# Constant fills on VectorE, and the input's buffers on the right-hand side of SBUF, in a hybrid decoder layer

## The chip, the cores and the metric

The kernel runs on one core of one Trainium2 chip. The metric is the device time of one execution in microseconds (us); lower is better. The engines are TensorE (PE in the profile, its weight loads PEld), VectorE (DVE), ScalarE (ACT), GpSimd (POOL) and SyncE (SP), which here issues nearly all DMAs.

## What is computed

One decoder layer over 512 tokens of width 1024, in float32. RMSNorm of the input x, one combined input projection `h @ w_in`, then three token mixers side by side (sparse attention over compressed, selected and window keys; a chunked spatial-gating MLP; RWKV-7 time mixing), each with a SiLU gate and its own output projection, merged by sigmoid gates, one output projection, a gated per-layer embedding, and a final RMSNorm. The part that the change touches is the beginning:

```
h = _rmsnorm(x, norm_g[i])
proj = h @ w_in[i]
nkc, nvc = ...                       # keys and values for compression, columns of proj
def _compress(kv, w1, w2, pe):
    blk = kv[:, idx] + pe            # blocks of 32 tokens, stride 16
    hid = silu(einsum('bnlgd,ldh->bngh', blk, w1))
    return einsum('bngh,hd->bngd', hid, w2)
```

## The kernel before

The kernel splits every float32 operand of the large projections into a high and a low half, so that each block takes three products: weights' high half by the activations' high half, the same weights by the activations' low half, and the weights' low half by the activations' high half. `wload` (L67 to L80) brings 256 KB of weights into a raw tile `wr` (4 buffers), ScalarE casts it to `wh` (L78), and VectorE or GpSimd subtracts to give `wl` (L79); `wh` and `wl` have 5 buffers each.

At the beginning GpSimd, and a little VectorE, fill constant tiles (L98 to L133, L186, L241 to L243). Meanwhile SP loads x in four tiles of 128 tokens (L182). For each tile ScalarE sums squares (L214, all four come first on ScalarE), VectorE and GpSimd form the scale `rsx` (L215, L216), VectorE scales the tile (L217), TensorE transposes it (L222, eight transposes), VectorE multiplies by the norm weights into `tg` (L224), ScalarE casts to `hH` (L225) and VectorE or GpSimd forms `hL` (L226). These buffers (`xs_`, `sqj`, `tg`) are the pool `xp`, which is closed after the last tile.

Next comes the projection of the compression keys and values (L250 to L265): two halves of 256 tokens, in each the keys and then the values (24 products of 256 columns each), into PSUM tiles `mm_ps` of which there are two buffers. After each, ScalarE copies the result out in four pieces (L264, L265) into `kc2`, a tile of the pool `cpp`, and that frees the PSUM tile. `cpp` is opened after `xp` was closed, on the same (left) side of SBUF, so it lies where `xp` lay. It also holds `w2t` and `w1t`, the weights of the compression MLP (L286, L291), and `blk`, its input (L294). `hid` (L298 to L301) is the product of `blk` and `w1t`.

After that come the first RWKV blocks (`rs_block`, L336 to L345: 24 products of 512 columns, out of the same two PSUM tiles), one block for the loras (number 12) and then the keys. Their weights are the fifth `wr` tile and those that follow. `Sb` and `wla`, which take the results, lie in a pool `shp` on the right-hand side. The tiles `hi`, `rT` and `w2r` of the RWKV stage lie in a pool `pr` high up on the left.

The kernel is written in one order, and a scheduler that simulates the engines sets the order of the instructions on each engine and puts in the waits; `issue_after` in the code adds some limits to it. Within one engine, and in SP's queue of DMA issues, everything then runs in that order. A tile that lies where another one lay waits until that one has been read for the last time.

Of the kernel before, what the change touches and what calls it, by code (L numbers as in the profile page):

```python
# [45 lines left out]
def hybrid_kernel(ctx, tc, x, p, norm_g, w_in, cmp_w1, cmp_w2, cmp_pe, sg_ln_g, sg_ln_b, sg_w, sg_b,  # L46
# [3 lines left out]
    V, S, G, PE, SY = nc.vector, nc.scalar, nc.gpsimd, nc.tensor, nc.sync  # L50
# [45 lines left out]
    identb = const.tile([128, 128], BF, name="identb")  # L96
    V.tensor_copy(identb, ident)
    trib = const.tile([128, 128], BF, name="trib")  # L98
    G.memset(trib, 0.0)
    G.affine_select(out=trib, in_=trib, pattern=[[-1, 128]], compare_op=OP.is_ge, fill=NEG, base=0,  # L100
                    channel_multiplier=1)
    cmask = const.tile([128, 4, 32], BF, name="cmask")
    G.memset(cmask, 0.0)
    G.affine_select(out=cmask, in_=cmask, pattern=[[128, 4], [-16, 32]], compare_op=OP.is_ge, fill=NEG,
                    base=-31, channel_multiplier=1)
    rowm = const.tile([128, 1], F32, name="rowm")
    G.memset(rowm, 1.0)
    G.affine_select(out=rowm, in_=rowm, pattern=[[0, 1]], compare_op=OP.is_ge, fill=0.0, base=-31,
                    channel_multiplier=1)
    gmask = const.tile([128, 2, 64], BF, name="gmask")  # L110
    G.memset(gmask, 1.0)
    for r in (0, 64):
        for ar in range(2):
            G.affine_select(out=gmask[r:r + 64, ar, :], in_=gmask[r:r + 64, ar, :], pattern=[[1, 64]],
                            compare_op=OP.is_ge, fill=0.0, base=ar - 1, channel_multiplier=-1)
    smask = const.tile([128, 8, 64], BF, name="smask")
    G.memset(smask, 1.0)
    G.memset(smask[:, :, 0:1], 0.0)
    tri = const.tile([128, 128], BF, name="tri")
    G.memset(tri, 1.0)  # L120
    G.affine_select(out=tri, in_=tri, pattern=[[1, 128]], compare_op=OP.is_ge, fill=0.0, base=0,
                    channel_multiplier=-1)
    mhalf = const.tile([128, 32], F32, name="mhalf")
    G.memset(mhalf, -0.5)
    bones = const.tile([128, 128], BF, name="bones")
    G.memset(bones, 0.0)
    G.memset(bones[0:64, 0:64], 1.0)
    G.memset(bones[64:128, 64:128], 1.0)
    hind = const.tile([128, 4, 8], F32, name="hind")
    G.memset(hind, 0.0)  # L130
    for q in range(4):
        for e in range(2):
            G.memset(hind[e * 64:e * 64 + 64, q, 2 * q + e:2 * q + e + 1], 1.0)  # L133

    ng8 = const.tile([8, 128], F32, name="ng8")
    ngp = const.tile([128, 8], F32, name="ngp")
# [34 lines left out]


    hcp = []
    xp_ctx = ExitStack()
    xp = xp_ctx.enter_context(tc.tile_pool(name="xp", bufs=1))
    xps = xp_ctx.enter_context(tc.tile_pool(name="xps", bufs=XP, space=PSUM))
    xs_ = xp.tile([128, 4, 1024], F32, name="xs_")
    ssx = xp.tile([128, 4], F32, name="ssx")
# [1 line left out]
    S.dma_start(ng8, norm_g[0].rearrange("(a b) -> a b", b=128))  # L180
    for t in range(4):
        SY.dma_start(xs_[:, t, :], x[t * 128:(t + 1) * 128, :])  # L182
    pw_ctx = ExitStack()
    pw = pw_ctx.enter_context(tc.tile_pool(name="pw", bufs=1, side="right"))
    prow = pw.tile([128, 128], F32, name="prow")
    G.memset(prow, 0.0)  # L186
    row = 0
    pls = []
    for nm, src in (("mu", rk_mu), ("w0", rk_w0), ("a0", rk_a0),
# [48 lines left out]
    kcst = const.tile([128, 2, 2, 32], R, name="kcst")  # L238
    vcst = const.tile([128, 2, 128], R, name="vcst")
    hm = const.tile([128, 4], F32, name="hm")  # L240
    G.memset(hm, 0.0)  # L241
    for hh in range(4):
        G.memset(hm[32 * hh:32 * hh + 32, hh:hh + 1], 1.0)  # L243
    cp_ctx = ExitStack()
    cpp = cp_ctx.enter_context(tc.tile_pool(name="cpp", bufs=1))
    cps = cp_ctx.enter_context(tc.tile_pool(name="cps", bufs=1, space=PSUM))
# [776 lines left out]
```

## Time and profile before

| | |
|---|---|
| time, median of 3 runs (lowest, highest) | 746.05 us (745.58, 747.11) |
| the profiled execution | 744.63 us |
| its span from first to last instruction | 742.8 us |
| busy share of TensorE (matmul), VectorE, ScalarE, GpSimd | 96%, 55%, 48%, 39% |
| share of TensorE in the chain of work that ended last | 88% |
| DMAs of the compression weights `w1t` | 4 of 512 KB |

The profile lists the busy time of each engine, the span in slices, the DMA queues, and the chain of work that ended last, followed back from the last instruction. With TensorE busy for 96% of the span, what matters are the places where it has no work or a lower clock. They lie mostly at the beginning, in the first 26 us, with some later ones of 0.4 to 2 us.

### The profile page before, as it was taken

The numbers are of one execution on the slowest core, as the hardware profiler recorded it, in microseconds if no ns is written. First come the engines' busy times: TensorE is split into PE (matmuls) and PEld (weight loads), VectorE is DVE, ScalarE is ACT, GpSimd is POOL, SyncE is SP. The second block draws the span as 40 slices with busy tenths as digits, with TensorE's granted clock in tenths as the row PEclk, the third lists the DMA queues.
The fourth block names the chain that finished last, engine by engine and source line by source line (L and its number), as shares of the span: only waits on it lengthen the run. The fifth ranks groups of instructions, "written<-read, shape, count | busy, mean of one in ns | idle before, by whom it ended". The sixth has DMA issues, their size and how long they took to land.

```text
span 742.8 us, 13074 instructions
## 1 busy us (share of the span) xinstructions
PE 714.5 (96%) x4941; PEld 606.7 (82%) x4941; DVE 408.6 (55%) x776; ACT 353.8 (48%) x743; POOL 287.0 (39%) x275
## 2 busy tenths in 40 slices
PE   4999999999999999989999999989999999999995
PEld 4888788999878987779877778867877888998995
DVE  6531587758843863565676565397555223226345
ACT  6554555542363342335565554576554333227453
POOL 6444640120220263300144345333445565356563
PEclk9999999999999999999999999999999999999999
DMA  5853122125536364427433212201228334132212
GB/s 194 188 140 100 48 81 71 41 85 146 156 105 224 101 184 117 116 86 232 124 97 103 58 43 71 71 16 42 53 62 268 96 91 127 59 114 72 80 63 114
DMA packets 106689, 78.73 MB, mean 106 GB/s; under 512 B 5569, under 2 KB 97282, under 8 KB 106626
## 3 DMA queue, kind: packets, MB, share of 16 engines
q1 hardware_dynamic: 105890, 75.27, 35.5%
q10 hardware_dynamic: 736, 2.63, 0.9%
q8 instruction: 39, 0.64, 0.4%
q14 instruction: 24, 0.20, 0.1%
HBM read 67.91 MB, written 9.96 MB: 105 GB/s over the span
## 4 chain that ended last, share of the span: by engine, by line
PE 88%; DVE 4%; ACT 2%; DMA 2%; issue 1%; POOL 1%; SPq 1%; ACTq 0%; POOLq 0%; DVEq 0%
PE mm_ps L62 70%; PE s_ps L62 3%; PE o_ps L62 2%; PE g_ps L62 2%; PE p_ps L875 2%; DMA w1t<-in_cmp_w_dram 1%; PE Yp L62 1%; DVE mx L861 1%; PE u_ps L62 1%; ACT wh L78 1%; PE xt_ps L222 1%; PE r_ps L62 1%; PE mx_ps L62 1%; DVE pl L879 1%; PE bk_ps L477 1%
## 5 line engine op out<-in xcount | busy, mean ns | idle before, releaser
L79 POOL TENSOR_TENSOR wl<-wr,wh 128x512 fp32r<-128x512 f32 x144 | 192.6, 1346 | 278.9 <-ACT wh L78 257.6
L78 ACT CAST wh<-wr 128x512 fp32r<-128x512 f32 (+1 forms) x194 | 119.4, 620 | 166.5 <-PE mm_ps L62 114.9
L62 PE MATMUL mm_ps<-hH,wh 128*128 128x512 f32 (+1 forms) x440 | 174.9, 398 | 3.3 <-ACT wh L78 1.9
L62 PE MATMUL mm_ps<-hL,wh 128*128 128x512 f32 (+1 forms) x440 | 171.6, 390 | 0.0
L62 PE MATMUL mm_ps<-hH,wl 128*128 128x512 f32 (+1 forms) x440 | 171.1, 389 | 0.0
L62 PEld LDWEIGHTS mm_ps<-hH,wh 128*128 128x128 f32 x440 | 83.5, 190 | 20.7 <-ACT wh L78 2.2
L62 PEld LDWEIGHTS mm_ps<-hH,wl 128*128 128x128 f32 x440 | 83.2, 189 | 17.4 <-issue 0.2
L62 PEld LDWEIGHTS mm_ps<-hL,wh 128*128 128x128 f32 x440 | 83.6, 190 | 16.5 <-issue 0.2
L62 PE MATMUL mm_ps<-wh,hL 128*128 128x256 f32 (+1 forms) x224 | 65.0, 291 | 0.0
L62 PE MATMUL mm_ps<-wh,hH 128*128 128x256 f32 (+1 forms) x224 | 63.8, 286 | 0.0
L62 PE MATMUL mm_ps<-wl,hH 128*128 128x256 f32 (+1 forms) x224 | 63.7, 285 | 0.0
L79 DVE TENSOR_TENSOR wl<-wr,wh 128x512 fp32r<-128x512 f32 (+1 forms) x50 | 38.0, 768 | 26.8 <-ACT wh L78 26.7
L62 PEld LDWEIGHTS mm_ps<-wh,hL 128*128 128x128 f32 x224 | 42.2, 188 | 1.1 <-issue 0.5
L62 PEld LDWEIGHTS mm_ps<-wh,hH 128*128 128x128 f32 x224 | 42.1, 188 | 1.2 <-issue 0.5
L62 PEld LDWEIGHTS mm_ps<-wl,hH 128*128 128x128 f32 x224 | 42.2, 188 | 0.5
L879 DVE TENSOR_TENSOR pl<-p_ps,ph 128x512 fp32r<-128x512 f32 x40 | 27.1, 685 | 25.7 <-ACT ph L878 25.6
L62 PE MATMUL mm_ps<-ysH,wh 128*128 128x512 f32 x96 | 38.6, 402 | 0.1
L62 PE MATMUL mm_ps<-ysL,wh 128*128 128x512 f32 x96 | 38.4, 400 | 0.2 <-DVE ysL L725 0.2
L62 PE MATMUL mm_ps<-ysH,wl 128*128 128x512 f32 x96 | 38.2, 398 | 0.0
L862 ACT ACTIVATE P<-s_ps,mx 128x512 f32<-128x512 f32 (+3 forms) x64 | 33.4, 531 | 7.9 <-DVE mx L861 5.5
L62 PE MATMUL mm_ps<-wh,mH 128*128 128x256 f32 x128 | 35.9, 286 | 0.0
L62 PE MATMUL mm_ps<-wl,hT 128*128 128x256 f32 x128 | 35.8, 281 | 0.0
(337 smaller groups left out, 1434.6 us busy)
## 6 DMA issues: line engine op xcount, KB each, us to landing
wr<-in_w_in_dram SPq DMA_DIRECT2D x130, 256.0 KB
wr<-in_w_branch_dram SPq DMA_DIRECT2D x24, 256.0 KB
wr<-in_w_o_dram SPq DMA_DIRECT2D x16, 256.0 KB
wr<-in_w_ple_gate_dram SPq DMA_DIRECT2D x16, 256.0 KB
xs__129<-in_x_dram SPq DMA_DIRECT2D x4, 512.0 KB
w1t<-in_cmp_w_dram SPq DMA_DIRECT2D x4, 512.0 KB
x<-in_x_dram ACTq DMA_DIRECT2D x4, 512.0 KB
out_dram<-x SPq DMA_DIRECT2D x8, 256.0 KB
```

The source lines that it names most:

```text
L62: return PE.matmul(o, a, b, start=start, stop=stop, **kw).ins
L78: S.copy(h[:, :m], raw[:, :m])
L79: ph_["l"].tensor_tensor(l[:, :m], raw[:, :m], f(h[:, :m]), OP.subtract)
L222: PE.transpose(ps[:, k, :], xs_[:, t, (4 * a + k) * 128:(4 * a + k + 1) * 128], ident)
L477: PE.transpose(ps[:, c - c0, :], bk[:, c, 0:2].rearrange("p s t -> p (s t)"), ident)
L861: V.tensor_reduce(mx[:, hh:hh + 1], s_ps[:, :W], axis=AX.X, op=OP.max, negate=True)
L862: S.activation(P[:, hh, :W], s_ps[:, :W], AF.Exp, bias=mx[:, hh:hh + 1], accum_out=sm[:, hh:hh + 1])
L875: PE.transpose(p_ps[:, hh * 128:hh * 128 + 128], P[:, hh, kt * 128:kt * 128 + 128], ident)
L879: V.tensor_tensor(pl, p_ps, f(ph), OP.subtract)
```

## The change

Of the fills of constants, 25 instructions (`trib`, `cmask`, `rowm`, `gmask`, `smask`, `tri`, `bones`, `hind`, `prow`, `hm`) are issued on VectorE instead of GpSimd. The pool `xp` of the input's buffers is placed on the right-hand side of SBUF, above the pool `pw` of `prow`, which is now opened before it. With that, `cpp` no longer lies where `xp` lay; `shp` and the upper part of `pr` do.

```
-    G.memset(trib, 0.0)
+    V.memset(trib, 0.0)
...
-    G.memset(hind, 0.0)
+    V.memset(hind, 0.0)
     for q in range(4):
         for e in range(2):
-            G.memset(hind[e * 64:e * 64 + 64, q, 2 * q + e:2 * q + e + 1], 1.0)
+            V.memset(hind[e * 64:e * 64 + 64, q, 2 * q + e:2 * q + e + 1], 1.0)
...
     hcp = []
+    pw_ctx = ExitStack()
+    pw = pw_ctx.enter_context(tc.tile_pool(name="pw", bufs=1, side="right"))
     xp_ctx = ExitStack()
-    xp = xp_ctx.enter_context(tc.tile_pool(name="xp", bufs=1))
+    xp = xp_ctx.enter_context(tc.tile_pool(name="xp", bufs=1, side="right"))
...
-    pw_ctx = ExitStack()
-    pw = pw_ctx.enter_context(tc.tile_pool(name="pw", bufs=1, side="right"))
     prow = pw.tile([128, 128], F32, name="prow")
-    G.memset(prow, 0.0)
+    V.memset(prow, 0.0)
...
-    G.memset(hm, 0.0)
+    V.memset(hm, 0.0)
     for hh in range(4):
-        G.memset(hm[32 * hh:32 * hh + 32, hh:hh + 1], 1.0)
+        V.memset(hm[32 * hh:32 * hh + 32, hh:hh + 1], 1.0)
```

The scheduler places instructions anew. On SP, in the queue of DMA issues just after the loads of the small parameters (`prow`), this is the difference, before with -, after with +; `w2t` and `w1t` are the compression weights, `wr` the weight tiles five to eight, `w2r` the lora weights:

```order
 L267 DMA prow<-in_cmp_pe_dram 16x64 x4
+L286 DMA w2t<-in_cmp_w_dram 128x64 x4
+L291 DMA w1t<-in_cmp_w_dram 64x16x128 x4
+L76 DMA wr<-in_w_in_dram 128x4x128 x4
 L368 DMA w2r<-in_rk_w_dram 64x512
 L369 DMA w2r<-in_rk_w_dram 64x512
 L368 DMA w2r<-in_rk_a_dram 64x512
 L369 DMA w2r<-in_rk_a_dram 64x512
-L76 DMA wr<-in_w_in_dram 128x4x128 x4
-L286 DMA w2t<-in_cmp_w_dram 128x64 x4
-L291 DMA w1t<-in_cmp_w_dram 64x16x128 x4
```

The eight issues of the compression weights stood behind the four of `wr` and now stand ahead of them, and the four of `w2r` have gone behind both.

On ScalarE, at the last casts of `hH` (difference, - before, + after); `wh_513` is the fifth weight tile, the first of block 12, and `mm_ps_293` the PSUM tile of the first product of the compression keys:

```order
 L225 CAST hH_121<-tg_219 128x4x128
 L225 CAST hH_121<-tg_233 128x4x128
-L78 CAST wh_513<-wr_512 128x512
 L225 CAST hH_121<-tg_242 128x4x128
 L264 COPY kc2_267<-mm_ps_293 64x256
```

The fifth weight tile's cast is gone from there; it stands further on in ScalarE's row, between the copies of the second product (`mm_ps_322`) and those of the third (`mm_ps_351`), where `wh_519` is the sixth weight tile (also of block 12), and `wh_552` and `wh_558` are the seventh and the eighth (of the next block):

```order
 L264 COPY kc2_267<-mm_ps_322 64x256
 L265 COPY kc2_267<-mm_ps_322 64x240
+L78 CAST wh_513<-wr_512 128x512
 L78 CAST wh_519<-wr_518 128x512
-L78 CAST wh_552<-wr_551 128x512
 L264 COPY kc2_267<-mm_ps_351 64x256
 L265 COPY kc2_267<-mm_ps_351 64x256
 L264 COPY kc2_267<-mm_ps_351 64x256
 L265 COPY kc2_267<-mm_ps_351 64x256
+L78 CAST wh_552<-wr_551 128x512
 L78 CAST wh_558<-wr_557 128x512
```

Both casts of block 12 now stand just ahead of the copies of the third product; the seventh tile's cast has moved behind those copies.

Further on, in the RWKV blocks and in the chunk loop of the state (L539 to L606), rows of VectorE, ScalarE and TensorE trade places over some instructions; from the attention on, the order is as before.

## Rows read from the trace of the kernel before

**Rows 1.** The page's first part: busy us (share of the span) xinstructions.

```profile
PE 714.5 (96%) x4941; PEld 606.7 (82%) x4941; DVE 408.6 (55%) x776; ACT 353.8 (48%) x743; POOL 287.0 (39%) x275
```

**Rows 2.** Timeline, start and length in us, start of VectorE and GpSimd, [idle before <-releaser].

```profile
0.97 0.48 DVE L393 MEMSET hi<- 128x512 f32 x1 [0.97 <-PEq L1011]
...
5.81 0.15 DVE L215 TENSOR_SCALAR rsx<-ssx 128x1 f32<-128x1 f32 x1 [2.23 <-ACT sqj L214]
...
6.36 0.49 POOL L243 MEMSET hm<- 32x1 f32 x4
...
6.94 0.56 POOL L216 TENSOR_TENSOR rsx<-rsx,mhalf 128x1 f32<-128x1 f32 x1
```

**Rows 3.** Timeline of TensorE around the compression projection.

```profile
25.33 0.39 PE L62 MATMUL mm_ps<-hH,wh 128*128 128x256 f32 x1 [1.40 <-ACT kc L265]
...
31.12 0.40 PE L62 MATMUL mm_ps<-hH,wh 128*128 128x512 f32 x1
...
38.84 3.68 PE L62 MATMUL hid<-w1t,blk 128*64 128x128 f32 x62 [0.22 <-DMA w1t<-in_cmp_w_dram]
```

**Rows 4.** Timeline of ScalarE: copies out of PSUM, and casts of weights.

```profile
23.80 0.37 ACT L264 COPY kc<-mm_ps 64x256 f32<-64x256 f32 x1 [1.71 <-DVE hL L226]
...
29.02 0.37 ACT L264 COPY kc<-mm_ps 64x256 f32<-64x256 f32 x1
...
39.36 0.62 ACT L78 CAST wh<-wr 128x512 fp32r<-128x512 f32 x1 [6.54 <-DMA wr<-in_w_in_dram]
40.26 1.32 ACT L78 CAST wh<-wr 128x512 fp32r<-128x512 f32 x2 [0.28 <-DMA wr<-in_w_in_dram]
```

**Rows 5.** Timeline of SP's queue: issues of DMAs, start and length of the issuing.

```profile
15.29 0.56 SPq L368 DMA_DIRECT2D w2r<-in_rk_w_dram  x1
...
17.86 3.92 SPq L76 DMA_DIRECT2D wr<-in_w_in_dram  x4
...
23.85 2.17 SPq L286 DMA_DIRECT2D w2t<-in_cmp_w_dram  x4
26.06 5.54 SPq L291 DMA_DIRECT2D w1t<-in_cmp_w_dram  x4
31.70 12.51 SPq L76 DMA_DIRECT2D wr<-in_w_in_dram  x7
```

**Rows 6.** The chain that ended last, the piece on w1t: start us, us, what.

```profile
28.91 9.80 DMA w1t<-in_cmp_w_dram
```

**Rows 7.** Stretches: us, length, TensorE clock (share of full), DMA share, GB/s.

```profile
28.00:29.00 1.00, 1.00 0.85 238
...
34.00:35.00 1.00, 1.00 1.24 215
...
39.00:40.00 1.00, 1.00 1.17 329
```

**Rows 8.** Stretches of TensorE: us, length, busy (instructions), clock, DMA share, GB/s.

```profile
8.00:10.00 2.00, 1.65 (x8) 1.00 1.13 338
...
14.00:15.00 1.00, 0.00 (x0) 1.00 0.05 10
...
16.00:17.00 1.00, 1.00 (x8) 0.51 0.30 93
...
19.00:20.00 1.00, 1.00 (x9) 0.78 0.96 241
```

**Rows 9.** Stretches of TensorE in the attention, the same columns.

```profile
544.00:545.00 1.00, 0.44 (x1) 1.00 0.00 0
545.00:546.00 1.00, 0.90 (x2) 0.54 0.00 0
...
548.00:549.00 1.00, 1.00 (x5) 0.75 0.00 0
```

**Rows 10.** Timeline of TensorE at the end of the chunk loop.

```profile
319.95 0.24 PE L62 MATMUL r_ps<-SV,Gt 128*64 128x64 f32 x1 [1.88 <-DVE SV L573]
```

More of the change, by code (lines that the diff above doesn't have):

```diff
@@ L102, in hybrid_kernel @@
     cmask = const.tile([128, 4, 32], BF, name="cmask")
-    G.memset(cmask, 0.0)
+    V.memset(cmask, 0.0)
     G.affine_select(out=cmask, in_=cmask, pattern=[[128, 4], [-16, 32]], compare_op=OP.is_ge, fill=NEG,
@@ L106, in hybrid_kernel @@
     rowm = const.tile([128, 1], F32, name="rowm")
-    G.memset(rowm, 1.0)
+    V.memset(rowm, 1.0)
     G.affine_select(out=rowm, in_=rowm, pattern=[[0, 1]], compare_op=OP.is_ge, fill=0.0, base=-31,
@@ L110, in hybrid_kernel @@
     gmask = const.tile([128, 2, 64], BF, name="gmask")
-    G.memset(gmask, 1.0)
+    V.memset(gmask, 1.0)
     for r in (0, 64):
@@ L116, in hybrid_kernel @@
     smask = const.tile([128, 8, 64], BF, name="smask")
-    G.memset(smask, 1.0)
-    G.memset(smask[:, :, 0:1], 0.0)
+    V.memset(smask, 1.0)
+    V.memset(smask[:, :, 0:1], 0.0)
     tri = const.tile([128, 128], BF, name="tri")
-    G.memset(tri, 1.0)
+    V.memset(tri, 1.0)
     G.affine_select(out=tri, in_=tri, pattern=[[1, 128]], compare_op=OP.is_ge, fill=0.0, base=0,
@@ L125, in hybrid_kernel @@
     bones = const.tile([128, 128], BF, name="bones")
-    G.memset(bones, 0.0)
-    G.memset(bones[0:64, 0:64], 1.0)
-    G.memset(bones[64:128, 64:128], 1.0)
+    V.memset(bones, 0.0)
+    V.memset(bones[0:64, 0:64], 1.0)
+    V.memset(bones[64:128, 64:128], 1.0)
     hind = const.tile([128, 4, 8], F32, name="hind")
-    G.memset(hind, 0.0)
+    V.memset(hind, 0.0)
     for q in range(4):
         for e in range(2):
-            G.memset(hind[e * 64:e * 64 + 64, q, 2 * q + e:2 * q + e + 1], 1.0)
+            V.memset(hind[e * 64:e * 64 + 64, q, 2 * q + e:2 * q + e + 1], 1.0)
     ng8 = const.tile([8, 128], F32, name="ng8")
```

## The prediction

> **What bounds the kernel now.** I read the busy shares first: TensorE computes for 96% of the span [rows 1], so a change can only pay where TensorE stands still or has half its clock, and only costs where it makes it stand. Then I read TensorE's timeline over the first 40 us. Three things are to be seen. TensorE stands for 1.40 us ahead of 25.33, from 23.93, until ScalarE has copied the first product of the compression keys out of PSUM [rows 3]. Those copies could start at 23.80 only: ScalarE had stood idle for 1.71 us, waiting for the last hL on VectorE, because kc2 lies on top of the input's buffers [rows 4]. And from 25.33 on TensorE runs without a gap to 31.12, where block 12 begins, and after that has one gap of 0.22 us, before hid, for the compression weights w1t [rows 3]. So before, the 2 MB of w1t come just in time. Last I read SP's queue, since the change turns over the order there [rows 5].
>
> **The change part by part. The fills.** 25 fills leave GpSimd. The last of them end at 6.85 (6.36 + 0.49), and the first rsx on GpSimd starts at 6.94, while its input is ready at 5.96 (5.81 + 0.15): at most 0.98 us are to be had [rows 2]. On VectorE, at GpSimd's price of 0.12 each (0.49 for four) with some more for the wide ones (0.48 for 512 float32 columns), 25 cost 3 to 4 us from 0.97 on and end before 5.81, so the wait for the first sum of squares hides them. If that cover failed, each microsecond over would delay the first tile by as much. The fills of hi and rT (0.48 each [rows 2]), which stood in that idle time, move behind the last hL, ahead of the parameters' copy; this makes some 1 us on VectorE, hidden because nothing reads the parameters before blk, which waits for kc2 much longer.
>
> **The input's buffers.** kc2 no longer waits for the last hL, so the 1.40 us of standing at 23.93 go. The second half of the compression projection takes 5.79 us (31.12 - 25.33 [rows 3]). Without the wait it would end at 29.7, and with all of the 0.98 us at 28.7. Up to here this is a gain of 1.4 to 2.4 us. The question is what is late next: block 12.
>
> **SP's queue, step by step.** w2t and w1t no longer wait for the input's buffers. They now follow the last load of small parameters, in the place where before w2r was issued at 15.29; w2t came at 23.85 and w1t at 26.06 [rows 5]. Everything about w1t so moves ahead by 8.56 us: its issues from 26.06 to 17.50, its landing from 38.71 (28.91 + 9.80 [rows 6]) to 30.15. That in itself helps nobody but hid's 0.22 us. But the transfer fills the DMA engines for some 10.7 us, from about 28.0 to 38.71 before, at 215 to 238 GB/s [rows 7], and a weight tile that was issued behind it at 31.70 [rows 5] landed only at 39.36, 0.65 us after it, the next at 40.26, 0.90 us later: ScalarE sat for both of them [rows 4]. The weight tiles five to eight were issued from 17.86 on before [rows 5], ahead of w1t, and now stand behind it. By those same distances the fifth lands at 30.15 + 0.65 = 30.80, the sixth at 31.70.
>
> **ScalarE's order.** Block 12 needs a free PSUM tile, the one of the third product (keys, second half). Its four copies now stand behind the casts of the fifth and sixth weight tile on ScalarE. So: the sixth lands at 31.70, cast 0.62 to 32.32, four copies of 0.37 [rows 4] with what lies between them 1.5 to 33.82, and some 0.1 for TensorE to see it: block 12 starts at 33.9 instead of 31.12 [rows 3]. That is +2.8 us, whatever the beginning gains: TensorE comes there at 28.7 to 29.7 and stands for 4.2 to 5.2 us. Queued behind the waiting casts are also the copies of the fourth product, which feed blk and hid; at 33.9 + 4.7 us (20 products ahead of the first hid) these are in time. GpSimd's wl of the fifth tile is done within 1.5 us of its cast, inside the wait. hid then no longer waits: -0.22. Sum so far: +2.6 us.
>
> **The clock.** After TensorE stood around 14 to 15, its granted clock was 0.5 (1.2 GHz of 2.4) from 16.0 to 19.4; a sparse stretch around 544 was followed by the same from 545.1 to 548.5 [rows 8, 9]. A wait of 4 to 5 us leaves more of a hole than either of these, so I expect one more such stretch. Both lasted 3.4 us; one more costs 1.7 us at most, and nothing where it lies inside the wait itself. I take 1.2, since it begins late in the wait or just after. The bounds are 0 and 1.7.
>
> **The rest.** In the RWKV blocks and the chunk loop instructions trade places. TensorE there has few gaps; the longest is 1.88 us at the end of the loop [rows 10]. It may vanish or double; I take 0, with 2 us to either side.
>
> **Sum.** +2.6 + 1.2 = +3.8 us on 744.63 of the profiled execution (742.8 of it the span). That execution lies 1.4 below the median of 746.05; what is added falls on both alike, so the forecast is 746.05 + 3.8 = 749.8 us.
>
> **The rivals.** Faster, by w1t's rate. The hold rests on w1t taking 10.7 us. x is moved at 338 GB/s at 8 to 10 us [rows 8], and weights behind w1t at 329 [rows 7]. If w1t, now issued into an empty queue, moved at 338, its 4 x 512 KB (2.10 MB) would take 6.2 us from 19.44 (28.0 - 8.56) and land at 25.6; the sixth tile at 27.2, the copies behind it done at 29.4. The point from which it decides: the sixth tile has to land by 27.5. Then block 12 starts at about 29.5, 1.6 us earlier, with hid's 0.22 a gain of 1.8: 744.2. Against it: nothing else was in the queue before either while w1t moved at 215 [rows 7]. The Trainium skill ("DMA: Bandwidth & Descriptors", Specifications) gives 512 bytes as the piece from which a transfer runs at line rate, and some 358 GB/s as the limit from HBM for one core; w1t's pieces are of 512 bytes, so by that page it would take 5.9 us (an estimate) and the sum would come out as this rival's. The trace disagrees, with 215 to 238 GB/s. I give it 0.08.
>
> A hold that is paid back later. The hold is as worked out, but the clock doesn't fall, or the gap of 1.88 us at the loop's end goes: 2.6 - 1.9 gives 746.7, and with some clock loss 747.5. It can't be read ahead, since it rests on many small moves; 0.14, within 0.2% of before.
>
> The change does nothing. If w1t were held by something else on its way (its turn on SP comes only after 24), all stays: 746. The order shows no such wait; 0.04.
>
> A larger loss. A second stretch of low clock, or a chunk loop that waits 2 us more: 751.5 to 754; 0.12.
>
> **How the numbers follow.** The forecast, 748.6 (no loss of clock) to 750.5, has 0.62. A measurement of this kernel can tell a difference of about 0.2%, 1.5 us, from none. Faster by more is the first rival: 0.08. Within 0.2% are the second and the third: 0.18. Slower by more: 0.62 + 0.12 = 0.74. For the range I leave out the first rival, a part of the third and the upper end of the last: 746.4 to 752.8.
>
> **What would show it.** In the profile after: w1t issued at about 17.5; the wait of 1.40 us for kc gone; ScalarE idle for some 5 us before the casts of the fifth and sixth weight tile, with the DMA as releaser, at about 31 and 32; TensorE standing from about 29 to 34 ahead of the first product of 512 columns, released by ScalarE; half the clock in or just after that wait; no wait for w1t before hid. I am wrong if the sixth tile is cast before 28, or if TensorE reaches block 12 without a wait. The clock's share is wrong if no stretch at 0.5 follows; the fills' share if the first rsx on GpSimd doesn't start near 6.0.

## The result, and the profile after

The changed kernel takes 752.84 us (median of 6 runs, 749.26 to 754.12), the kernel before 746.28 us beside it (745.58 to 747.11): a ratio of 1.0081, 95% interval 1.0057 to 1.0105. It is slower by 6.6 us; the forecast was 749.8, slower by 3.8, with a range up to 752.8. As a time the median lies 0.04 us above the range's end; by the ratio, on the 746.05 us that the forecast started from, it is 752.1. Either way it lies above the 748.6 to 750.5 that the forecast held most likely. The profiled execution took 754.01 us, with a span of 752.2. Both kernels were profiled a second time later (e12_before, e13_after below), which matters, since the first profile of the changed kernel shows more than its median does.

The busy line of the page, to be held against [rows 1]: VectorE has gained the fills, GpSimd has lost them, and TensorE's share is the same, 96%, of a span that is 9.4 us longer.

```profile
PE 721.3 (96%) x4941; PEld 611.2 (81%) x4941; DVE 410.1 (55%) x801; ACT 353.9 (47%) x743; POOL 283.4 (38%) x250
```

GpSimd's timeline at the start (start, duration, engine, line, operation; in brackets the idle time ahead and what ended it). The first rsx starts at 6.00 instead of 6.94 [rows 2], as forecast:

```profile
6.00 0.56 POOL L216 TENSOR_TENSOR rsx<-rsx,mhalf 128x1 f32<-128x1 f32 x1 [2.43 <-DVE rsx L215]
```

SP's queue of DMA issues, the answer to [rows 5] (start, time over which the issues run, how many):

```profile
15.89 1.84 SPq L286 DMA_DIRECT2D w2t<-in_cmp_w_dram  x4
17.77 4.96 SPq L291 DMA_DIRECT2D w1t<-in_cmp_w_dram  x4
22.84 5.75 SPq L76 DMA_DIRECT2D wr<-in_w_in_dram  x4
```

w1t is issued 8.3 us sooner than before, and the weights of block 12, which were issued from 17.86, now come behind it, from 22.84.

ScalarE's timeline, the answer to [rows 4]. It sits for 5.88 us until the fifth weight tile has landed, casts it and the sixth, and only then copies the third product out of PSUM (four copies, the first and the last shown):

```profile
25.55 0.35 ACT L265 COPY kc<-mm_ps 64x240 f32<-64x240 f32 x1
31.79 0.62 ACT L78 CAST wh<-wr 128x512 fp32r<-128x512 f32 x1 [5.88 <-DMA wr<-in_w_in_dram]
32.81 0.62 ACT L78 CAST wh<-wr 128x512 fp32r<-128x512 f32 x1 [0.41 <-DMA wr<-in_w_in_dram]
33.45 0.36 ACT L264 COPY kc<-mm_ps 64x256 f32<-64x256 f32 x1
...
34.59 0.37 ACT L265 COPY kc<-mm_ps 64x256 f32<-64x256 f32 x1
```

TensorE, the answer to [rows 3]. The wait of 1.40 us at 23.93 is gone; in its place TensorE stands for 4.81 us ahead of block 12, and after it the products of 512 columns follow each other at half speed:

```profile
35.01 0.80 PE L62 MATMUL mm_ps<-hH,wh 128*128 128x512 f32 x1 [4.81 <-ACT kc L265]
35.60 0.63 PE L62 MATMUL mm_ps<-hL,wh 128*128 128x512 f32 x1
...
39.79 0.39 PE L62 MATMUL mm_ps<-hH,wl 128*128 128x512 f32 x1
```

TensorE in stretches of 1 us (stretch, its length, busy time, instructions, granted clock, DMA share, GB/s), to be read against [rows 8]: half the clock from 32.8 to 39.7, of which the part from 35.01 on is paid for.

```profile
32.00:33.00 1.00, 0.00 (x0) 0.92 0.99 255
35.00:36.00 1.00, 0.99 (x2) 0.50 0.88 246
39.00:40.00 1.00, 1.00 (x4) 0.66 0.81 185
```

### The profile page after: what moved, and what is told of

The parts are those of the page before. It is cut to its first block, busy times and chain, and to the rows that moved or that the text cites. A ratio compares the mean times of both kernels' runs of the same rounds, so it can differ in the third digit from the quotient of the medians.

```text
span 752.2 us, 13078 instructions
## 1 busy us (share of the span) xinstructions
PE 721.3 (96%) x4941; PEld 611.2 (81%) x4941; DVE 410.1 (55%) x801; ACT 353.9 (47%) x743; POOL 283.4 (38%) x250
## 4 chain that ended last, share of the span: by engine, by line
PE 88%; DVE 5%; DMA 2%; ACT 2%; issue 1%; SPq 1%; POOL 0%; ACTq 0%; POOLq 0%; DVEq 0%
PE mm_ps L62 70%; PE s_ps L62 3%; PE o_ps L62 2%; DMA wr<-in_w_in_dram 2%; PE g_ps L62 2%; PE p_ps L875 2%; PE Yp L62 1%; PE u_ps L62 1%; DVE mx L861 1%; PE mx_ps L62 1%; PE r_ps L62 1%; DVE pl L879 1%; PE bk_ps L477 1%; PE hid L62 1%; PE st_ps L62 0%
## 5 line engine op out<-in xcount | busy, mean ns | idle before, releaser
L62 PE MATMUL mm_ps<-hL,wh 128*128 128x512 f32 (+1 forms) x440 | 173.4, 394 | 0.8 <-POOL hL L226 0.8
L62 PE MATMUL mm_ps<-hH,wl 128*128 128x512 f32 (+1 forms) x440 | 173.3, 394 | 0.2 <-DVE wl L79 0.2
L79 DVE TENSOR_TENSOR wl<-wr,wh 128x512 fp32r<-128x512 f32 (+1 forms) x50 | 35.8, 726 | 30.0 <-ACT wh L78 26.8
```

What stands on the lines that cost most here:

```text
L62: return PE.matmul(o, a, b, start=start, stop=stop, **kw).ins
L79: ph_["l"].tensor_tensor(l[:, :m], raw[:, :m], f(h[:, :m]), OP.subtract)
```

## The experiments

Times are medians; each ratio is to runs of the kernel before on the same chip, and since it comes from all runs and not from the two medians, it can differ from their quotient by about 0.1%. "Block 12" is the start of the first product of 512 columns on TensorE, "slp" that of the one product that needs the compression's hid and th, and "ss_ps to iv_ps" the length of the loop over the four row groups of the RWKV stage, from its first product ahead (sums of squares) to the first one behind it (the inverse). These three columns are read from the one profile of each run.

| | time | ratio (95%) | block 12 | slp | ss_ps to iv_ps |
|---|---|---|---|---|---|
| before / e12_before | 746.28 / 745.91 | 0.9994 (0.9984, 1.0004) | 31.12 / 31.13 | 47.7 / 47.9 | 135.2 / 135.1 |
| after / e13_after | 752.84 / 752.51 | 1.0081 (1.0057, 1.0105) / 1.0084 (1.0063, 1.0104) | 35.01 / 33.90 | 53.4 / 51.8 | 136.9 / 136.9 |
| e1_fills | 747.40 | 1.0008 (0.9994, 1.0022) | 32.51 | 48.8 | 135.2 |
| e2_side | 750.35 | 1.0060 (1.0043, 1.0076) | 33.59 | 52.3 | 135.1 |
| e3_behind | 747.64 | 1.0019 (1.0008, 1.0031) | 28.90 | 46.9 | 136.9 |
| e4_copies | 749.02 | 1.0046 (1.0030, 1.0062) | 30.72 | 48.7 | 136.9 |
| e5_half | 746.28 | 0.9996 (0.9987, 1.0005) | 30.30 | 47.0 | 136.9 |
| e6_pin | 750.87 | 1.0050 (1.0035, 1.0064) | 34.40 | 52.3 | 135.0 |
| e8_behind_pin_th | 744.80 | 0.9978 (0.9965, 0.9990) | 30.57 | 46.8 | 135.0 |
| e9_glue | 743.32 | 0.9950 (0.9934, 0.9966) | 31.14 | 47.4 | 137.1 |
| e10_all | 743.28 | 0.9958 (0.9946, 0.9970) | 30.26 | 46.5 | 135.5 |
| e11_aglue | 748.51 | 1.0019 (0.9998, 1.0040) | 34.13 | 53.1 | 137.1 |

**e1_fills: the fills alone.** Against the changed kernel, the input's buffers are back on the left:

```
-    xp = xp_ctx.enter_context(tc.tile_pool(name="xp", bufs=1, side="right"))
+    xp = xp_ctx.enter_context(tc.tile_pool(name="xp", bufs=1))
```

> The fills of constants alone on VectorE; the input's buffers stay on the left as before. Theory (block 12 waits for weights queued behind w1t, and for copies queued behind their casts on ScalarE): no wait before block 12, since w1t still waits for the input's buffers; the first rsx on GpSimd at about 6.0 instead of 6.94, block 12 at 30.2 to 31.1, time 745.3 to 746.3 (0 to -1 us). Rival (the fills themselves cost, by delaying VectorE's first work): 2 us or more slower than before. Rival (the loss sits in the instructions that traded places in the chunk loop): as before, unless the clock falls at a new place.

No difference from before that the times show. The first rsx does come sooner, but the copies of the first product still wait for the last hL on VectorE, here until 23.66 (23.80 before [rows 4]), and TensorE now stands for 2.07 us instead of 1.40: what the start gains, it waits out there. ScalarE and TensorE:

```profile
23.66 0.36 ACT L264 COPY kc<-mm_ps 64x256 f32<-64x256 f32 x1 [1.89 <-DVE hL L226]
...
25.19 0.39 PE L62 MATMUL mm_ps<-hH,wh 128*128 128x256 f32 x1 [2.07 <-ACT kc L265]
```

Block 12 was expected at 30.2 to 31.1 and starts at 32.51. Behind that wait the granted clock is at half from 26.6 to 30.0 us, so the second half of the projection takes 7.32 us instead of 5.79. TensorE in one stretch of 1 us (columns as above):

```profile
27.00:28.00 1.00, 1.00 (x7) 0.50 0.58 174
```

A wait of that length isn't always followed by this. e12_before, a second profile of the kernel before, waits 2.27 us at the same place and keeps the full clock until 321 us:

```profile
25.34 0.39 PE L62 MATMUL mm_ps<-hH,wh 128*128 128x256 f32 x1 [2.27 <-ACT kc L265]
```

**e2_side: the buffers alone.** The 25 fills are back on GpSimd (one of them shown):

```
-    V.memset(trib, 0.0)
+    G.memset(trib, 0.0)
```

> The input's buffers alone on the right; the fills stay on GpSimd. Theory: all of the loss is here: w1t issued ahead of the weight tiles five to eight, block 12 at about 35 instead of 31.1, ScalarE idle some 5 us before the fifth tile's cast, a stretch at half the clock around it, time 751 to 754. Rival (the fills cost): 744 to 746.5.

This part carries 4.5 of the 6.6 us, most of the loss, where I had expected all of it; slp is 4.6 us later than before. ScalarE sits until the weights behind w1t have landed, and TensorE stands as in the changed kernel:

```profile
30.44 0.62 ACT L78 CAST wh<-wr 128x512 fp32r<-128x512 f32 x1 [5.14 <-DMA wr<-in_w_in_dram]
...
33.59 0.80 PE L62 MATMUL mm_ps<-hH,wh 128*128 128x512 f32 x1 [4.12 <-ACT kc L265]
```

The loop over the four row groups takes 135.1 us here, as before, and 136.9 in the changed kernel. So the remaining 2 us are neither part by itself: the scheduler turns the loop over only with both.

**e3_behind: w1t behind the weights.** The weights of blocks 12 and 4 are loaded ahead of w2t and w1t:

```
+    for b in (12, 4):
+        wpre[O_RS + 128 * b] = wparts([(w_in, O_RS + 128 * b, 128)], 8)
+    with tc.issue_after(wdma[-1]):
         w2t = cpp.tile([128, 2, 128], F32, name="w2t")
...
+            w1t = cpp.tile([128, 16, 128], F32, tag="w1t", name="w1t", bufs=2)
```

> The changed kernel, but w2t and w1t are issued on SP only behind the weight tiles five to eight. Theory: the wait of 4.8 us before block 12 goes, and the 1.4 us for kc stays gone: block 12 at 29.3 to 30.2, w1t lands at 36 to 37, at most 1 us of waiting for it before hid, no stretch at half the clock there; time 743.5 to 745.5, faster than before by 1 to 2.5 us. Rival (the loss sits in later instructions that traded places, or in their clock): still 750 or more, although block 12 starts on time.

The hold is gone: TensorE runs into block 12 without a wait at 28.90, 2.2 us ahead of before. The casts of the fifth, sixth and seventh weight tile still stand ahead of the third product's copies, but the fifth waits only 0.64 us for its weights and the others not at all (the seventh's cast and the first of the copies):

```profile
26.19 0.62 ACT L81 CAST wh<-wr 128x512 fp32r<-128x512 f32 x1 [0.82 <-PE mm_ps L62]
26.84 0.36 ACT L267 COPY kc<-mm_ps 64x256 f32<-64x256 f32 x1
```

But slp is only 0.8 us ahead, because it now waits for th, whose Tanh stands behind the casts of the lora weights on ScalarE. TensorE's wait, and ScalarE's row:

```profile
46.91 0.33 PE L312 MATMUL slp<-ident,th 128*128 128x128 f32 x1 [1.59 <-DVE th L310]
```

```profile
43.17 1.12 ACT L377 CAST w2H<-w2r 128x512 fp32r<-128x512 f32 x2
44.32 1.26 ACT L379 CAST wlS<-wla 64x512 fp32r<-64x512 f32 x2
45.49 0.26 ACT L309 ACTIVATE th<-hid 128x128 f32<-128x128 f32 x1
```

Then the loop loses 1.7 to 1.8 us, as in the changed kernel, and the whole, expected at 743.5 to 745.5, is 1.8 us slower than before (5.2 faster than the changed kernel), although the loss at the start is undone.

**e4_copies: the copies ahead of the casts.** The queue stays as changed; on ScalarE the casts for block 12 are kept behind the copies of the third product:

```
+                    kcp.append(S.copy(kc2[64:128, kv, g, c0 - sh:c0 + 240], ps[g * 64:g * 64 + 64, 16 - sh:256]).ins)
...
-    for b in (12, 4, 5, 6, 7):
+    with tc.issue_after(kcp[5]):
+        rs_block(12)
+    for b in (4, 5, 6, 7):
```

> The changed kernel with its order of DMAs, but on ScalarE the four copies of the third product are put ahead of the casts of the weight tiles five and six. Theory: the wait has two parts, the landing of the fifth tile behind w1t (31.8) and the sixth tile with four copies behind it (2.6 us more). Without the second part block 12 starts at 32.5 to 32.7 instead of 35.0; with the clock falling as before the time is 2 to 3 us less than that of the changed kernel, 749.5 to 751. Rival (the DMAs alone set it, ScalarE's order is hidden): block 12 at 34 to 35, time unchanged at 752 to 753.

Block 12 begins at 30.72 with w1t still ahead of its weights in the queue. ScalarE copies first and sits afterwards, when TensorE has work:

```profile
29.22 0.37 ACT L266 COPY kc<-mm_ps 64x256 f32<-64x256 f32 x1
29.61 0.62 ACT L78 CAST wh<-wr 128x512 fp32r<-128x512 f32 x1
31.75 0.62 ACT L78 CAST wh<-wr 128x512 fp32r<-128x512 f32 x1 [1.52 <-DMA wr<-in_w_in_dram]
```

slp is about 0.9 us later than before, instead of 5.7. So with the copies ahead the late weights cost about a microsecond; this is not their clean price, since this profile also has half the clock from 15.3 to 22.2 us. The rest of the hold needs the order on ScalarE, which made everything behind the casts as late as the weights. The forecast for block 12, 32.5 to 32.7, took the landing of the fifth tile from the first profile of the changed kernel; here its cast, at 29.61, waits for nothing. The loop's loss is still there (136.9).

**e5_half: half of w1t.** The second w1t tile and its two loads are left out; the compression's values are computed with the keys' weights.

```
-        w1t = cpp.tile([128, 16, 128], F32, tag="w1t", name="w1t", bufs=2)
-        for lh in range(2):
+        if kv == 0:
+            w1t = cpp.tile([128, 16, 128], F32, tag="w1t", name="w1t", bufs=2)
+        for lh in range(2 if kv == 0 else 0):
```

> The changed kernel with one tile w1t instead of two: the second half of the compression (the values) uses the keys' weights, so 1 MB of w1t, which took 4.96 us of the queue's issue time, is 0.5 MB, and its transfer into the queue ahead of the weights of block 12 is half as long. The scheduler also puts one of the four late casts of ScalarE behind the first product's copies. The theory that the 4.81 us wait of TensorE ahead of block 12 is ScalarE's casts standing behind w1t in the queue expects wr5 to wr8 to be issued some 2.5 us sooner (20.3 instead of 22.84), ScalarE's cast of wh5 no longer to wait 5.88 us but 2 to 4, block 12 at about 32 instead of 35.01, and with it 749 to 750.5 against 752.8 for the changed kernel. If the wait were set by something else on ScalarE (the order of copies behind casts alone, whatever w1t's size), block 12 would stay within 0.5 us of 35.0 and the time within 1 us of 752.8. The loop over the four row groups has the changed kernel's order, so the 1.8 us lost there stay in both theories.

The hold is gone altogether, not by half. My number missed because I halved the 4.96 us of issue time, while the two issues that are left take 1.56, so that the weights of block 12 are issued 4.6 us sooner, not 2.5:

```profile
16.59 1.56 SPq L292 DMA_DIRECT2D w1t<-in_cmp_w_dram  x2
18.25 4.41 SPq L76 DMA_DIRECT2D wr<-in_w_in_dram  x4
```

```profile
25.06 0.62 ACT L78 CAST wh<-wr 128x512 fp32r<-128x512 f32 x1 [1.48 <-DMA wr<-in_w_in_dram]
...
27.20 1.14 ACT L78 CAST wh<-wr 128x512 fp32r<-128x512 f32 x2
28.38 0.37 ACT L264 COPY kc<-mm_ps 64x256 f32<-64x256 f32 x1
```

The fifth tile's cast waits 1.48 us instead of 5.88, at a time when TensorE is busy, and the casts of the sixth and the seventh, still ahead of the third product's copies, wait for nothing. So the rival, that the order sets the hold whatever the size of w1t, is out. e3_behind and this run take away the late weights and leave casts ahead of the copies; e4_copies takes away that order and leaves the weights behind w1t. In none of the three does TensorE stand ahead of block 12: the hold needs both.

**e12_before and e13_after: a second profile of both.** No edit.

> The kernel before once more, unchanged, for a second profile. Its first profile has TensorE's granted clock at 0.5 for two stretches of 3.4 us (from 16 and from 545 us), the changed kernel's has 6.8 us at 32 to 39, 3.4 us at 224 and 6.8 us at 329. If the falls at about 220 and 320 us come and go from one execution to the next, whatever the kernel, this profile has one or both of them (at 215 to 222 and 315 to 325), with the time within the spread of this kernel's runs (744.4 to 749.3). If they belong to the change, this profile has neither, as the first.

> The changed kernel once more, unchanged, for a second profile. If the low clock at 32 to 39 us is the answer to the 4.8 us in which TensorE stands still ahead of block 12, it is there again at the same place (within 2 us), and block 12 again starts at about 35 us; of the falls at 224 and 329 us it is open whether they are there. If it was chance, the stretch 32 to 39 runs at full clock this time and slp is some 2 us earlier.

The times repeat (0.9994; 1.0084). In e13_after the wait ahead of block 12 is there again, with half the clock behind it. ScalarE (casts of the fifth and the sixth tile), TensorE, and TensorE's stretches (columns as above):

```profile
29.22 0.62 ACT L78 CAST wh<-wr 128x512 fp32r<-128x512 f32 x1 [3.30 <-DMA wr<-in_w_in_dram]
31.71 0.62 ACT L78 CAST wh<-wr 128x512 fp32r<-128x512 f32 x1 [1.86 <-DMA wr<-in_w_in_dram]
```

```profile
33.90 0.50 PE L62 MATMUL mm_ps<-hH,wh 128*128 128x512 f32 x1 [3.70 <-ACT kc L265]
```

```profile
34.00:35.00 1.00, 1.00 (x4) 0.71 0.28 46
...
37.00:38.00 1.00, 1.00 (x4) 0.58 0.04 2
```

The queue as a whole stands 1.5 us earlier than in the first profile (w1t from 16.32 instead of 17.77), and after the wait's end there are 3.4 us at half the clock (34.4 to 37.8) instead of 4.7.

Two later falls, which only the changed kernel's first profile showed, are now told apart. The one at 329 is in e12_before as well, for 6.8 us:

```profile
321.00:322.00 1.00, 1.00 (x16) 0.50 0.45 170
327.00:328.00 1.00, 1.00 (x4) 0.61 0.23 90
```

It is in every profile of these experiments and missing only in the first of the kernel before, so it is no part of the change. The one at 222 to 228 is in both profiles of the changed kernel and in neither of the kernel before. But e1_fills, e3_behind, e9_glue, e10_all and e11_aglue have one there too (between 215 and 231), while e2_side, e4_copies, e5_half, e6_pin and e8_behind_pin_th have none; whether it belongs to the change stays open.

**e6_pin: VectorE's order in the loop put back.** In this loop TensorE forms the products `g_ps` in eight groups of eight, four for each half of 64 rows, into two PSUM tiles, one for each half; VectorE evacuates both into `Gt` (L472).

```
+        with behind(q - 1, 1):
-        V.tensor_tensor(kkn, kkn, ta, OP.mult)
+            V.tensor_tensor(kkn, kkn, ta, OP.mult)
```

(and the same for three more steps; `behind(q, n)` is an `issue_after` on the n-th evacuation into Gt of row group q)

> The changed kernel with one thing put back: in the loop over the four row groups, VectorE's order is tied so that the products' evacuation into Gt goes ahead of the next row group's steps, as in the kernel before. TensorE's order then has three of the eight groups of g_ps products in a row, as before, instead of two. The theory that the 1.8 us that the changed kernel loses between the sums of squares (ss_ps) and the inverse (iv_ps) come from that order expects 135.2 us for that stretch instead of 136.9, g_ps products busy 15.6 us instead of 17.0, and 751 against 752.8 for the changed kernel; the start up to the product of the compression (slp at 53.4) stays as it is. The rival, that the 1.8 us come from the early part (memory that comes free later, the shifted transfers) and not from the order, expects 136.9 us there and the time of the changed kernel.

As the theory had it: 135.0 us for the loop, with the start as in the changed kernel, and 2 us less. The 2 us rest on the loop's length; the times alone are not quite enough, since the ratio's interval (up to 1.0064) just overlaps those of the changed kernel (from 1.0057 and 1.0063). The row of all g_ps products between 70 or 72 and 216 us (engine, operation, tiles, count of records | busy us, mean ns | idle ahead), in before, after, e6_pin, and, for the next run, e9_glue:

```profile
L62 PE MATMUL g_ps<-AR,bk 64*128 64x128 f32 x128 | 15.6, 285 | 0.0
```

```profile
L62 PE MATMUL g_ps<-AR,bk 64*128 64x128 f32 x128 | 17.0, 285 | 0.2
```

```profile
L62 PE MATMUL g_ps<-AR,bk 64*128 64x128 f32 x128 | 15.9, 285 | 0.0
```

```profile
L62 PE MATMUL g_ps<-AR,bk 64*128 64x128 f32 x128 | 9.8, 285 | 0.0
```

The mean of one record is the same everywhere, the busy time isn't (a product leaves two records). The kernel before issues three of the eight groups in a row, with the two 64-row halves in turn, and five split into halves; the changed kernel two and six. TensorE's timeline of before has a whole group (16 records) and a half of one (8 records):

```profile
105.89 1.16 PE L62 MATMUL g_ps<-AR,bk 64*128 64x128 f32 x16
...
115.80 1.16 PE L62 MATMUL g_ps<-AR,bk 64*128 64x128 f32 x8
```

A half takes as long as the whole. My reading is that a group is split where its second PSUM tile comes free later than its first; the evacuation that frees it (Gt, L472) was put behind two other steps on VectorE in the changed kernel (start, duration, line; before, where it comes ahead of both, and after):

```profile
104.47 1.28 DVE L472 TENSOR_TENSOR Gt<-g_ps,gmask 128x512 f32<-128x512 f32 x2
```

```profile
110.96 0.74 DVE L342 SCALAR_TENSOR_TENSOR AR<-mm_ps,omu,Sb 128x512 f32<-128x512 f32 x1
111.62 1.74 DVE L449 TENSOR_TENSOR kkn<-kkn,ta 128x512 f32<-128x512 f32 x1
113.29 1.27 DVE L472 TENSOR_TENSOR Gt<-g_ps,gmask 128x512 f32<-128x512 f32 x2
```

**e9_glue: the kernel before, with all groups whole.**

```
-            gps = [rps.tile([128, 4, 2, 64], F32, tag="g", name="g_ps", bufs=2) for e in range(2)]
+            gp2 = rps.tile([128, 2, 4, 2, 64], F32, tag="g", name="g_ps")
+            gps = [gp2[:, e] for e in range(2)]
```

(the other users of these two PSUM banks, `ss_ps`, `hi_ps`, `rT_ps` and `bo`, take the same two-bank tile)

> The kernel before, with one edit in the loop over the four row groups: the two accumulators of a group of g_ps products (one for each 64-row half) are one tile of two banks instead of two tiles of one, so both come free together and the scheduler issues all eight groups of eight products in a row, the two halves in turn; in the kernel before three groups stand so and five are split into halves. In the trace of before a whole group takes 1.10 us and a half of one 1.08. If the halves run beside each other only when they alternate, five split groups cost 5 x 1.06 = 5.3 us, the products' busy time falls from 15.6 to about 9 us, and the time to some 741 to 743 if nothing else becomes late. The rival: TensorE isn't the bound there, since with one pair of accumulators a group now waits for VectorE's evacuation of the group ahead of it; then the busy time falls just as far but the stretch between ss_ps and iv_ps stays at 135 us or grows, and the time is 745 to 748.

Faster than before by 0.5%, about 3 us (743.3, just above the 741 to 743 expected), with the products busy 9.8 us instead of 15.6. So it was the two separate tiles that split the groups, and splitting costs time, at the end too. Of the 5.8 us only half arrives: from the first ss_ps to the last r_ps it is 247.2 us instead of 250.0. TensorE is idle for 3.3 us of that instead of 2.6, and this profile has half the clock from 219.7 to 223.2 us, which the kernel before hasn't; where the rest of the other half goes wasn't followed. The loop's own length, 137.1 us, doesn't count against it, since more of the later products are done inside it (938 records of TensorE's products instead of 903).

**e11_aglue: the changed kernel, with all groups whole.** The same edit on the changed kernel.

> The changed kernel (752.8 us) with e9_glue's edit alone; the queue and ScalarE's order at the start stay as they are, so block 12 stays at about 35 us and slp at about 53. If the loss in the loop of the four row groups is the sixth split group of g_ps products, the edit wins here what it won in the kernel before and the loss as well: 752.8 - 2.9 - 1.8, about 748, with the products busy 9.8 us instead of 17.0. If the loss in the loop has another cause (VectorE's order by itself), the edit wins 2.9 us only and the time is about 750.

748.5 as forecast, with the products busy 9.8 us, and 4.3 us below the changed kernel, against 2.9 in the kernel before. This agrees with one split group more in the changed kernel; the runs of this kernel spread from 743.8 to 751.8, so the difference of 1.4 us between the two gains isn't firm by itself.

**e8_behind_pin_th and e10_all: what is to be had.** e3_behind with e6_pin's order, and with th ahead of the lora casts on ScalarE:

```
-    S.activation(th, hid, AF.Tanh, scale=0.5)
+    tha = S.activation(th, hid, AF.Tanh, scale=0.5).ins
...
+        with tc.issue_after(tha), tc.issue_after(thv):
```

> The changed kernel with all three of the suspected losses taken away at once: the weights of blocks 12 and 4 ahead of w2t and w1t in the queue (as in e3_behind), the compression's Tanh and its VectorE step ahead of the casts of w2H and wlS on ScalarE (e3_behind waited 1.59 us for them), and VectorE's order in the loop as in e6_pin. If the loss has these three places, the times add: e3_behind's 747.6, less 1.6 for the wait, less 1.7 for the loop: about 744.5, 1 to 2 us under the kernel before. If the loss in the loop or the wait only moves on to the next late thing, the time stays within 1 us of e3_behind's 747.6. Milestones: block 12 at 28.9, slp at 45.3 instead of 46.9, first iv_ps at 204 instead of 207.2.

744.8, against 744.5 expected, and below the kernel before with an interval that leaves 1 out (by 0.1% to 0.35%). The three edits together undo more than the loss. The closeness to 744.5 is partly luck: block 12 was expected at 28.9 and starts at 30.57, slp at 45.3 and starts at 46.8, because this profile has half the clock from 15.1 to 22.0 us, which e3_behind's hasn't. The wait ahead of slp is gone, and so is the loop's loss (135.0); what the start lacks is made up behind the loop, where this profile is 1.4 us shorter than e3_behind's, with half the clock from 322.3 to 325.7 instead of 217.2 to 220.6 and 323.0 to 329.8. e10_all adds e9_glue's edit:

> e8_behind_pin_th (744.8 us) with e9_glue's edit (one tile of two banks for a group of g_ps products, which took the kernel before from 746.2 to 743.3, with the products busy 9.8 us instead of 15.6). If the two losses are separate, the times add: 744.8 - 2.9 = 741.9, and the products are busy 9.8 us instead of 15.9. If the gain of e9_glue came from time that e8_behind_pin_th has already won in the same loop (the evacuation into Gt ahead of the next row group's steps), the time stays within 1 us of the better of the two, 743 to 745.

743.28, not 741.9: no better than e9_glue alone. The start's gain is there (the first ss_ps at 69.9, against 70.8 in e9_glue); what is missing is the gain of the glued groups: from the first ss_ps to the last r_ps it takes 249.6 us, against 247.2 in e9_glue and 250.2 in e8_behind_pin_th, although the products are busy 9.8 us here too. TensorE is idle for 4.9 us of that instead of 3.3, and the clock is at half for 6.8 us in it (from 215.8) instead of 3.4. What brings the longer idling on, these runs don't show.

## Why the prediction was right, and where it fell short

The starts of six products divide the time into parts (rounded, so a sum can differ by 0.1). Forecast, then what the changed kernel lost there in the first pair of profiles (before, after) and in the second (e12_before, e13_after):

| part | forecast | first pair | second pair |
|---|---|---|---|
| start to block 12 (the hold) | +2.8 | +3.9 | +2.8 |
| block 12 to first hid (the clock) | +1.2 | +2.0 | +1.4 |
| first hid to slp (w1t's wait) | -0.2 | -0.1 | -0.3 |
| slp to first ss_ps | 0 | 0 | 0 |
| first ss_ps to first iv_ps (the loop) | 0 | +1.7 | +1.7 |
| first iv_ps to last r_ps | 0 | +1.0 | +0.7 |
| last r_ps to the end | 0 | +0.8 | +0.4 |
| sum | +3.8 | +9.4 | +6.6 |

The rows behind the loop's line in the second pair, e12_before and then e13_after (duration in ns: least, median, most; after the comma the first and the last start):

```profile
L62 PE MATMUL ss_ps<-hind,sq x64: 202/203/223, 71.3 to 73.1; 128*64 128x8 f32 x64
L62 PE MATMUL iv_ps<-itmp,Gt x128: 191/191/212, 206.4 to 208.4; 32*32 32x32 f32 x128
```

```profile
L62 PE MATMUL ss_ps<-hind,sq x64: 202/203/223, 75.1 to 77.0; 128*64 128x8 f32 x64
L62 PE MATMUL iv_ps<-itmp,Gt x128: 191/191/212, 212.0 to 214.0; 32*32 32x32 f32 x128
```

The second pair's sum is that of the medians, 6.6.

**The fills.** Right that VectorE hides them: they end at 3.70, ahead of the first sum of squares at 5.76. Right also that the gain of up to 0.98 us at the start would not arrive; e1_fills shows it swallowed by the wait for hL, and in the changed kernel by the hold.

**The input's buffers.** Right: the wait of 1.40 us is gone, and nothing is won by it.

**SP's queue and ScalarE's order.** Right in kind and, in the second pair, in size: cast of the sixth tile at 31.71 (forecast: lands at 31.70), block 12 at 33.90 (forecast 33.9). That it fits to 0.01 us is luck: w1t was issued 1.2 us sooner than forecast (16.32, not 17.50), the fifth tile's cast came 1.6 us before its forecast landing (29.22, not 30.80), and the sixth came 2.5 us behind the fifth instead of 0.9. In the first profile all of this lay 1.1 us or more later, since the queue was late from the first load on; over the five profiles with the hold block 12 starts at 33.59 to 35.01. e3_behind, e4_copies and e5_half confirm that both the late weights and the order on ScalarE are needed for it. The order is less new than the prediction says: the kernel before, too, casts the sixth and the seventh tile, at 26.94 and 28.37, ahead of the third product's copies at 29.02 [rows 4], but there the weights had landed in time. e2_side shows that the hold comes from the buffers' side, not from the fills.

**The rival of w1t's rate** fell: from 20 to 30 us the queue moved 225 to 255 GB/s, with nothing else ahead, close to the 215 to 238 of the trace of before. TensorE's stretches of 2 us with the DMA rate in the last column:

```profile
20.00:22.00 2.00, 2.00 (x20) 1.00 1.11 255
22.00:24.00 2.00, 2.00 (x20) 1.00 1.24 225
```

**The clock.** Right that a stretch at 1.2 GHz follows the wait; the price was 1.4 to 2.0 us where I took 1.2 with a bound of 1.7. The bound was too low for the first profile, where the low clock lasted 6.8 us, not 3.4: I had taken the length from the two stretches of before and had not allowed for two in a row. Every profile with the wait ahead of block 12 has such a stretch right there (after, e2_side, e6_pin, e11_aglue, e13_after; the waits are 3.65 to 5.32 us, the prices 1.4 to 2.5), and none without it. The premise that I took from the start of the trace of before is weaker than I made it: e12_before stands there too, for 1.42 us ahead of 15.24 (before: 1.94 ahead of 15.22), and no low clock follows.

**The rest.** This is the step that failed: I took 0, with 2 us to either side, for the loop and the chunk loop. The loop alone cost 1.7 to 1.8 us, in all five profiles with this order of the loop (after, e13_after, e3_behind, e4_copies, e5_half) and in none of the four with the old one (before, e12_before, e1_fills, e2_side). That is one sum of its kind that could have been made ahead: in the trace of before a half group of g_ps products takes the time of a whole one, and the new order of TensorE splits one more. The term stood inside its bounds, and with it the sum reached no further than the range's end, but the value taken for it was the middle, not what the rows said.

What lies behind the loop is less sure to be the change's. The part from the first iv_ps to the last r_ps takes 115.9 to 116.5 us in the profiles with a fall of the clock at 217 to 228 (after, e13_after, e1_fills, e3_behind) and 114.4 to 115.3 in those without (before, e12_before, e2_side, e4_copies, e5_half, e6_pin, e8_behind_pin_th), whichever order the loop has: the 0.7 to 1.0 us there go with that fall. The part from the last r_ps to the end varies from 421.7 to 423.9 us over all profiles, with no order by kernel, so its 0.4 to 0.8 us are not shown to be the change's.

**The larger loss**, my rival at 0.12 with 751.5 to 754, has the number of the result, and the range reached so far up only because of this rival. Its mechanisms were only half right: a second stretch of low clock in one of two profiles, and 2 us more, but in the loop of the row groups and not as a wait at the chunk loop's end.

## What to carry to other kernels

When a wait for memory is removed, look for what else was held back by it: here the freed transfer of 2 MB went ahead of 1 MB that was needed sooner, and a cast waiting for that 1 MB stood ahead of PSUM copies on its engine, so an early start turned into 4 us of standing and 1.4 to 2 us of half clock. Keep an instruction that waits for a DMA behind those on its engine that free PSUM, or the DMA ahead of its rivals; either was enough. And where a change lets a scheduler trade places far from the edit, count in the new order what is known to be dear in the old trace, split groups for one, instead of putting zero for it.

## What the runs showed of the hardware

Products with 64 rows of contraction ran beside each other only when the two halves of the array came in turn: 16 records in turn take 1.16 us, 8 of one half the same 1.16. The Trainium skill ("TensorE: Matmul & The Clock Gate", Part 3: Packing small matmuls — row/col tiling) says that products in distinct row groups run concurrently; the whole groups agree, and the split ones show what is lost when the order pulls them apart.

Standing for a few microseconds and a fall of the granted clock to half went together only in part: five waits of 3.65 to 5.32 us were all followed by 3.4 or 6.8 us at half, a wait of 2.07 us (e1_fills) by 3.4 us, and one of 2.27 us at the same place (e12_before) by none.

The same program's DMA queue can stand 1.5 us earlier or later from one execution to the next from its first loads on (the four loads of x took 2.59 us to issue in after, 1.81 in e13_after); here that was worth 1.1 us at block 12. And stretches at half the clock of 3.4 or 6.8 us came and went at the same few places from profile to profile of one kernel: the fall at about 321 is missing in before and 6.8 us long in e12_before, with 742.8 and 744.0 us of span.
